# A two-layer hybrid decoder trunk: another order of the heads' projections, single-tile groups at the start, and SP's queue in the planner

## The chip, the cores and the metric

One core of a Trainium2 chip runs the whole program. The metric is the device time in microseconds of one execution. Engine names: PE is TensorE (PEld its weight loads), DVE is VectorE, ACT is ScalarE, POOL is GpSimd, SP is SyncE, on whose queue all loads and stores of this kernel are issued.

## The reference

Sequence 256, width 2048, two layers. For each layer the reference computes

```python
mod = silu(c) @ w_ada[l] + b_ada[l]            # 6 vectors: shift, scale, gate of the mixer, then of the FFN
h = rms_norm(x, ln_mix[l]) * (1 + sc_m) + sh_m
proj = h @ w_in[l]                             # q, k, v, z, b, a of 8 DeltaNet heads; q, k, v of attention
dn_out = gated_deltanet(...)                   # conv, chunked recurrence with a triangular inverse per 64 steps
at_out = sliding_window_attention_sinks(...)   # 16 query heads, 2 key/value heads
x = x + gt_m * (concat(dn_out, at_out) @ w_out[l])
h = rms_norm(x, ln_ffn[l]) * (1 + sc_f) + sh_f
x = x + gt_f * ((silu(gate) * up) @ w_down[l]) # gate, up = h @ w_gate_up[l]
```

and ends with an RMS norm. All inputs are float32.

## The kernel before

x stays in SBUF, transposed: 16 tiles `x[:, k, :]` (k tiles) of 128 channels x 256 positions. Every weight block of 128x128 is split by ACT into a rounded part `wh` and by DVE or POOL into a rest `wl` (`Weights.split`), each activation likewise into two halves (`act`), and a product of a block is three matmuls of 256 columns (`mm3`, for the mixer) or one of 512 and one of 256 (`mm2`, for the FFN and the second product of it).

The order of the work is fixed while the program is built. `Timed` keeps an estimated clock for each engine and prices every recorded instruction; `Steps.run` lets the generators (one for each head, each attention pair, each addition to x) record their next step when the estimate says that its input is there; `Timed.dma` estimates when a load lands, and `Timed.carry` records the small transfers of 8 KB (`qi<-mc`, `uc<-ui`) that rearrange the 16x16 blocks for the inverses. The engines and SP then execute their queues in the recorded order; a step that was recorded too soon makes its engine wait, with all that stands behind it.

The stages, with the names that the change touches:

- **Start of layer 0.** `Ada.products` computes the modulation's shift and scale (m = 0, 1) on PE: loads `wx` of 128x1024, each multiplied in 32-row groups with the columns of silu(c) in `cs`; `finish` turns the result (copy `th`, product with `sel`) and adds it to `mod`. `first_normed` squares x (`kq`), sums the squares (`R`), makes the norm's factor (`ms`, `n2r`, `do`, `ry`), and then for each k tile `gain`, `cv` and the two halves of `act`. Meanwhile 28 early projections (`EARLY`) are accumulated k group by k group (`GROUPS`, now (0, 2), (2, 4), (4, 6), (6, 10)); `keep` stores or adds each partial sum in SBUF. The last group, (10, 16), is done in the next stage. A shift and scale for two k tiles come out of 8 loads.
- **Heads (mix0, mix1).** The projections in the order of `JOBS`: "ak", "av" and "aq" for attention, "k", "q", "v", "z" for the heads. `scores` prepares a head; after the fourth head of a batch (`BATCH` = 4) `inverses` carries `mc` to `qi`, inverts, and carries `ui` to `uc`, 8 transfers each time; `delta` then runs the recurrence of one head, a chain of small products (`con,U`, `W,B`, `y,U`, `U,yn`, `con,vT`, ...) with a DVE or ACT step after each. The projection "v" of head h waits until head h - 2 has got past its `con,vT` step ("mid").
- **Output projection**, with `add_x` adding into x, and the **FFN**. In all stages from the middle of mix0 on, DVE also multiplies the remaining modulation weights (`wada`, `Ada.rows`), 1.2 us for each of 256 loads.

In the order before, each head's k, q and one aq follow each other to the end:

```python
for _h in range(H):
    JOBS += [("v", _h), ("z", _h)]
    for _n in range(BATCH, H):
        if _n - BATCH == _h:
            JOBS += [("k", _n), ("q", _n), ("aq", _n)]
```

Of the kernel before, what the change touches and what calls it, by code (L numbers as in the profile page):

```python
# [23 lines left out]
ALU = mybir.AluOpType  # L24
# [3 lines left out]
KT = D // 128  # L28
# [7 lines left out]
AHEAD, BATCH = 2, 4  # L36
JOBS = [("ak", 0), ("av", 0)] + [("aq", h) for h in range(AHEAD)]
for _h in range(BATCH):
    JOBS += [("k", _h), ("q", _h)] + [("aq", AHEAD + _h // 2)] * (_h % 2)
for _h in range(H):  # L40
    JOBS += [("v", _h), ("z", _h)]
    for _n in range(BATCH, H):
        if _n - BATCH == _h:
            JOBS += [("k", _n), ("q", _n), ("aq", _n)]
# [56 lines left out]
class Timed:  # L101
# [5 lines left out]
    def __init__(self, nc):  # L107
        self.nc, self.floor, self.end, self.count = nc, 0, 0, 0
        self.form = None
        self.clock = {e: 0 for e in ("tensor", "vector", "scalar", "gpsimd")}  # L110
        for e in self.clock:
            setattr(self, e, Engine(self, e))
        self.loads = 0
# [69 lines left out]


JOIN = 4, 2
# [139 lines left out]
class Weights:  # L325
# [60 lines left out]
    def split(self, upto, force=True):  # L386
        nc, b = self.nc, self.b
        while self.nsplit < min(upto, len(self.parts)):
# [3 lines left out]
            eng = "gpsimd" if free and not ffn else "vector"  # L392
# [41 lines left out]
def trunk(tc, xT, bada, c, c_col, par, con, w_in, w_ba, w_ada0, w_ada, w_out, w_gu, w_dn, out):  # L434
    nc = Timed(tc.nc)
    with (
# [38 lines left out]
        for l in range(L):  # L475
            if l == 0:
                for lo, hi in GROUPS[:-1]:
                    n = 8 // (hi - lo)
                    for i in range(0, len(EARLY), n):
                        W.across(w_in[0, i : i + n], lo, hi)  # L480
# [26 lines left out]
        class Ada:  # L507
            BUFS = 3

            def __init__(self):  # L510

                self.todo = [(0, m, j, i) for j in range(8) for m in (1, 0) for i in range(4)]
# [30 lines left out]
            def load(self):  # L543
# [4 lines left out]
                if self.nload < self.cols:  # L548
                    src = w_ada0[COLS.index(m), k, i]
# [5 lines left out]
            def products(self):  # L555
# [3 lines left out]
                for n in range(self.cols):  # L559
                    _, m, j, i = self.todo[n]  # L560
                    size = 1 if m in (1, 0) else 8
                    at = j % size
                    begin, end = i == at == 0, i == 3 and at == size - 1
# [20 lines left out]
                    if end:  # L584
                        self.groups += 1
                        S.add(self.finish(m, j - at, size, to, half), 0)
# [20 lines left out]
            def finish(self, m, j, size, to, half):  # L607
# [6 lines left out]
                for i in range(2):  # L614
# [6 lines left out]
                at = mod[:, 0, m * 16 + 2 * j : m * 16 + 2 * (j + size)].rearrange("p (j i) -> p i j", i=2)  # L621
                nc.vector.tensor_tensor(
                    out=at, in0=at, in1=q[:, 0 : 2 * size].rearrange("p (i j) -> p i j", i=2), op=ALU.add
                )
                b.give("psm")
                self.have.update((0, m, k) for k in range(2 * j, 2 * (j + size)))
# [55 lines left out]
        for n, upto in zip([0] + [len(EARLY) * (hi - lo) // 8 for lo, hi in GROUPS[:-1]], [hi for _, hi in GROUPS]):  # L682
# [233 lines left out]
        def first_normed(x_at, ln, hs):  # L916
            acc = b.t("R", [128, 2, T], bufs=1)
            for i in range(KT // 2):
                yield from b.take("kq", A_)
                nc.floor = max(nc.floor, x_at[i // 2])  # L920
                sq = b.t("kq", [128, 2, T])
                nc.scalar.activation(out=sq, in_=x[:, 2 * i : 2 * i + 2, :], func=AF.Square)
                yield D_
# [4 lines left out]
                b.give("kq")  # L928
# [389 lines left out]
        def inverses(bt, ui):  # L1318
# [8 lines left out]
            nc.end += 7500  # L1327
# [42 lines left out]
            nc.end += 7500  # L1370
# [381 lines left out]
```

## Time and profile before

| | us |
|---|---|
| median of 3 runs | 2565.11 (2564.06 to 2567.55) |
| the profiled execution | 2560.1 |
| its span, first to last instruction | 2558.4 |
| PE busy in the span | 2454.5 |
| DVE / ACT / POOL busy | 1853.5 / 1295.8 / 433.7 |
| mean clock granted to PE | 0.98 of 2.4 GHz |

The profiled execution's time lies 1.7 us above its span and 5.0 us below the median of the runs. The start of layer 0 takes the first 200 us, mix0 lasts to about 505 us, its output projection to 583 us, the FFN to 1335 us, mix1 with its output projection to 1797 us, and the second FFN to the end. "Busy" counts an instruction from its start to its end, at either clock, so time in which PE works at half its clock does not show as idle.

### The profile page before, as it was taken

What the parts mean: (1) busy time and instruction counts of PE and PEld (TensorE: products, weight loads), DVE (VectorE), ACT (ScalarE), POOL (GpSimd) and SP (SyncE); (2) the same over time, 40 slices, a digit from 0 to 9 for tenths busy, and PEclk for the clock granted to TensorE, in tenths of its full rate; (3) what the DMA queues carried; (4) which work ended last, traced back from release to release, by engine and by line L of the source; (5) the groups of instructions that cost most, each with busy time, mean ns of one, the idle gap of its engine ahead of it and who ended that gap; (6) DMA issues with size and microseconds to landing.
All of it is one profiled execution on the core that took longest, in us unless ns stands there. A gap on an engine that the chain in (4) does not pass through costs nothing. (4 is left out here: it accounts for less than half of the span.)

```text
span 2558.4 us, 45650 instructions
## 1 busy us (share of the span) xinstructions
PE 2454.5 (96%) x16878; PEld 2166.9 (85%) x16878; DVE 1853.5 (72%) x3823; ACT 1295.8 (51%) x2760; POOL 433.7 (17%) x389
## 2 busy tenths in 40 slices
PE   6999998988999999999999999899899999999998
PEld 5887787987888888888888899899788888888887
DVE  3758767778777999999987876655877765555565
ACT  4346563535555445555445655454555544555553
POOL 2333232670000000000004333246000000000000
PEclk9999998999999999999999999899999999999999
DMA  9987565776777999999983333346677766555564
GB/s 358 340 300 257 191 231 194 248 267 205 251 256 262 341 354 348 354 349 347 333 293 132 133 130 127 119 160 225 214 255 247 240 190 191 190 190 190 184 189 138
DMA packets 192786, 609.05 MB, mean 238 GB/s; under 512 B 27825, under 2 KB 39217, under 8 KB 192561
## 3 DMA queue, kind: packets, MB, share of 16 engines
q1 hardware_dynamic: 192562, 606.14, 68.8%
q8 instruction: 132, 2.16, 0.3%
q14 instruction: 92, 0.75, 0.1%
HBM read 603.44 MB, written 2.10 MB: 237 GB/s over the span
## 5 line engine op out<-in xcount | busy, mean ns | idle before, releaser
L172 ACT CAST wh<-w 128x512 fp32r<-128x512 f32 x1532 | 896.0, 604 | 475.4 <-PE psm L172 163.0
L172 DVE TENSOR_TENSOR wl<-w,wh 128x512 fp32r<-128x512 f32 (+1 forms) x1293 | 860.8, 683 | 249.7 <-ACT wh L172 237.3
L172 PE MATMUL pr<-act,wh 128*128 128x512 f32 x2816 | 883.5, 394 | 7.6 <-DVE kq L172 4.4
L172 PE MATMUL pm<-act,wh 128*128 128x256 f32 x3328 | 643.5, 293 | 15.6 <-DVE x L172 6.8
L172 PEld LDWEIGHTS pr<-act,wl 128*128 128x128 f32 x2816 | 531.8, 189 | 124.1 <-DVE wl L172 1.4
L172 PE MATMUL pr<-act,wl 128*128 128x256 f32 x2816 | 561.6, 280 | 0.9 <-DVE wl L172 0.9
L172 PEld LDWEIGHTS pm<-act,wh 128*128 128x128 f32 x3328 | 520.9, 192 | 39.0 <-issue 22.7
L172 POOL TENSOR_TENSOR wl<-w,wh 128x512 fp32r<-128x512 f32 (+1 forms) x239 | 331.9, 1398 | 1181.7 <-ACT wh L172 1097.1
L172 PE MATMUL pm<-act,wl 128*128 128x256 f32 x1664 | 474.1, 285 | 0.2 <-POOL wl L172 0.2
L172 PEld LDWEIGHTS pr<-act,wh 128*128 128x128 f32 x2816 | 433.5, 189 | 10.3 <-DVE kq L172 5.0
L172 DVE CUSTOM_DVE_ANT_0 wada<-wada,cs 128x1024 f32<-128x1024 f32 x256 | 330.1, 1290 | 123.0 <-DMA wada<-w_ada 122.8
L172 PE MATMUL psm<-act,wh 128*128 128x512 f32 (+1 forms) x1280 | 363.8, 362 | 1.4 <-DVE act L172 1.2
L172 PEld LDWEIGHTS pm<-act,wl 128*128 128x128 f32 x1664 | 319.5, 192 | 0.4 <-POOL wl L172 0.4
L172 PEld LDWEIGHTS psm<-act,wl 128*128 128x128 f32 x1088 | 205.2, 189 | 39.0
L172 PE MATMUL psm<-act,wl 128*128 128x256 f32 x1088 | 233.3, 281 | 0.0
L172 PEld LDWEIGHTS psm<-act,wh 128*128 128x128 f32 x1280 | 201.4, 189 | 5.8 <-issue 3.7
L172 PE MATMUL psm<-mid,wh 128*128 128x512 f32 x512 | 169.7, 392 | 0.0
L172 POOL TENSOR_TENSOR n2r<-ms,halfc 128x2 f32<-128x2 f32 x5 | 3.5, 690 | 798.4 <-DVE ms L172 798.4
L172 ACT COPY kq<-pr 128x512 f32<-128x512 f32 x88 | 51.4, 587 | 167.2 <-PE pr L172 167.2
L172 PEld LDWEIGHTS psm<-mid,wl 128*128 128x128 f32 x512 | 96.1, 188 | 21.6
L172 DVE TENSOR_TENSOR kq<-pr,kq 128x512 f32<-128x512 f32 x88 | 60.5, 688 | 72.3 <-ACT kq L172 72.3
L172 DVE SCALAR_TENSOR_TENSOR x<-psm,mod,x 128x256 f32<-128x256 f32 x128 | 61.8, 483 | 57.4 <-PE psm L172 54.9
(188 smaller groups left out, 1984.3 us busy)
## 6 DMA issues: line engine op xcount, KB each, us to landing
w<-w_gu SPq DMA_DIRECT2D x352, 512.0 KB
wada<-w_ada SPq DMA_DIRECT2D x320, 512.0 KB
w<-w_in SPq DMA_DIRECT2D x130, 512.0 KB
w<-w_dn SPq DMA_DIRECT2D x128, 512.0 KB
wx<-w_ada SPq DMA_DIRECT2D x64, 512.0 KB
w<-w_out SPq DMA_DIRECT2D x64, 512.0 KB
w<-w_dn SPq DMA_DIRECT2D x64, 384.0 KB
w<-w_in SPq DMA_DIRECT2D x28, 384.0 KB
```

Source lines behind the costliest of these rows:

```text
L172: return f(*a, **k)
```

## The change

It does five things.

1. `JOBS` is written out as a string. Now k, q of the second batch come together sooner (k6 q6 k7 q7 before v3) and aq5, aq6, aq7 stand after z3, between k7 q7 and v4 z4; aq0 and aq1 are no longer both among the first four.
2. `Timed.dma` keeps a time of SP's queue: 400 ns for each load there, and 380 bytes per ns for the transfers in place of 350. `Timed.carry` puts 650 ns on the same queue for each small transfer, and the carried data is there 2000 ns after the last; the fixed 7500 ns after a set of eight are gone.
3. The first modulation goes k tile by k tile: `wx` holds half of the rows for one tile of 128 channels, and a shift and scale for one k tile come out of 4 loads. A load is now multiplied by 8 products of 128 columns (before, 4 of 256). The first four loads are multiplied one by one as they come, later ones four at a time.
4. `GROUPS` begins with (0, 1), (1, 2) in place of (0, 2): two passes over the 28 projections with one k tile each. Their weights come in loads of eight tiles x 128 columns, in pieces of 512 bytes (before, 1 KB).
5. `first_normed` records the squares and their sums without yielding in between, and POOL takes no split before the first product.

```diff
-GROUPS = ((0, 2), (2, 4), (4, 6), (6, 10), (10, 16))
+BATCH = 4
+ORDER = (
+    "ak av aq0 k0 q0 k1 q1 aq1 k2 q2 k3 q3 aq2 aq3 v0 z0 v1 z1 k4 q4 aq4 k5 q5 v2 z2 k6 q6 k7 q7 v3 z3 "
+    "aq5 aq6 aq7 v4 z4 v5 z5 v6 z6 v7 z7 "
+)
+GROUPS = ((0, 1), (1, 2), (2, 4), (4, 6), (6, 10), (10, 16))
...
-        self.loads = max(self.loads, self.clock["tensor"], after) + n / 350
+        self.queue = max(self.queue, self.clock["tensor"], after) + 400
+        self.loads = max(self.loads, self.queue) + n / 380
...
-        self.end = max(self.end, self.floor)
+        self.queue = max(self.queue, self.floor) + 650
+        self.end = max(self.end, self.queue + 2000)
...
-            eng = "gpsimd" if free and not ffn else "vector"
+            eng = "gpsimd" if free and not ffn and self.p else "vector"
...
-                self.todo = [(0, m, j, i) for j in range(8) for m in (1, 0) for i in range(4)]
+                self.todo = [(0, m, k, i) for k in range(KT) for m in (1, 0) for i in range(2)]
...
-                    join = JOIN[n >= self.first]
+                    join = 1 if n < 4 else 4 if early else 2
...
-                    for r in range(4):
-                        c0 = (i * 4 + r) * 32 + 31 - at
+                    size = 128 if early else T
+                    cols = to[:, m * 128 : m * 128 + 128] if early else to
+                    for r in range(1024 // size):
+                        c0 = (i * 1024 // size + r) * 32 + 31 - at
                         nc.tensor.matmul(
-                            to[r * 32 : r * 32 + 32, :], cs[:, c0 : c0 + 32], w[:, r * T : r * T + T], start=begin, stop=end
+                            cols[r % 4 * 32 : r % 4 * 32 + 32, :], cs[:, c0 : c0 + 32], w[:, r * size : r * size + size],
+                            start=(i == 0 and r < 4) if early else begin, stop=(i == 1 and r >= 4) if early else end,
                         )
...
             for i in range(KT // 2):
-                yield from b.take("kq", A_)
-                nc.floor = max(nc.floor, x_at[i // 2])
+                nc.floor = x_at[i // 2]
                 sq = b.t("kq", [128, 2, T])
                 nc.scalar.activation(out=sq, in_=x[:, 2 * i : 2 * i + 2, :], func=AF.Square)
-                yield D_
+                nc.floor = nc.end
...
-            nc.end += 7500
```

Three places on PE show how the order moves. The first is PE's queue from its beginning (`wx` is a load of the modulation, `R` the sum of squares, `do` the norm's factor, `th` the turned row, `act,wh` a projection). Before:

```order
L172 MATMUL psm_111<-wx_93,cs_69 32x256 x4
L172 MATMUL psm_111<-wx_95,cs_69 32x256 x4
L172 MATMUL psm_111<-wx_97,cs_69 32x256 x4
L172 MATMUL psm_111<-wx_99,cs_69 32x256 x4
L172 MATMUL psm_169<-con_67,th_166 128x1 x2
L172 MATMUL psm_172<-con_67,R_112 128x1 x4
L172 MATMUL psm_184<-do_182,con_67 128x256
L172 MATMUL psm_111<-wx_101,cs_69 32x256 x4
L172 MATMUL psm_111<-wx_103,cs_69 32x256 x4
L172 MATMUL psm_111<-wx_105,cs_69 32x256 x4
L172 MATMUL psm_111<-wx_107,cs_69 32x256 x4
L172 MATMUL psm_231<-con_67,th_229 128x1 x2
```

Now:

```order
L172 MATMUL psm_117<-wx_93,cs_69 32x128 x8
L172 MATMUL psm_155<-con_67,R_118 128x1 x4
L172 MATMUL psm_117<-wx_95,cs_69 32x128 x8
L172 MATMUL psm_176<-do_174,con_67 128x256
L172 MATMUL psm_117<-wx_97,cs_69 32x128 x8
L172 MATMUL psm_117<-wx_99,cs_69 32x128 x8
L172 MATMUL psm_213<-con_67,th_203 128x1 x2
L172 MATMUL pm_92<-act_228,wh_205 128x256 x2
L172 MATMUL pm_92<-act_228,wl_206 128x256
L172 MATMUL pm_234<-act_228,wh_205 128x256 x2
```

The norm's products moved in between the first four loads' products, and the first projection stands behind four loads in place of eight.

The second is PE's queue in layer 1 where heads 4 and 5 begin their recurrence (`con,U` is its first step; `act,wh` and `act,wl` are projections). Before:

```order
L172 MATMUL pm_20201<-act_16371,wl_20155 128x256
L172 MATMUL psm_20311<-con_67,U_20305 128x128 x2
L172 MATMUL psm_20314<-con_67,U_20308 128x128 x2
L172 MATMUL psm_20322<-W_20317,B_18116 128x64 x2
L172 MATMUL psm_20325<-W_20319,B_18759 128x64 x2
L172 MATMUL psm_20331<-y_3671_16390,U_20305 128x64
L172 MATMUL psm_20331<-U_20305,y_3671_16390 128x64
L172 MATMUL psm_20331<-y_3671_16390,U_20305 128x64
L172 MATMUL psm_20331<-U_20305,y_3671_16390 128x64
L172 MATMUL psm_20336<-y_3672_16391,U_20308 128x64
L172 MATMUL psm_20336<-U_20308,y_3672_16391 128x64
```

This goes on for 25 more rows of heads 4 and 5 without a projection. Now, for head 4:

```order
L172 MATMUL pm_20151<-act_16423,wl_20035 128x256
L172 MATMUL psm_20182<-con_67,U_20164 128x128 x2
L172 MATMUL pm_20151<-act_16444,wh_20056 128x256 x2
...
L172 MATMUL pm_20151<-act_16555,wl_20081 128x256
L172 MATMUL psm_20219<-W_20199,B_18740 128x64 x2
L172 MATMUL pm_20151<-act_16576,wh_20080 128x256 x2
L172 MATMUL pm_20151<-act_16576,wl_20081 128x256
...
L172 MATMUL pm_20151<-act_16664,wl_20113 128x256
L172 MATMUL psm_20252<-y_3700_16704,U_20164 128x64
L172 MATMUL psm_20252<-U_20164,y_3700_16704 128x64
L172 MATMUL psm_20252<-y_3700_16704,U_20164 128x64
```

Between any two steps of the head stand products of a projection, and head 5 no longer goes in step with head 4. Layer 0 shows the same at its heads 4 and 5.

The third is PE's queue in layer 0 at heads 0 and 1 (`wada,cs` are modulation products). Before, the last projection's product stands in the middle of head 0's steps:

```order
L172 MATMUL pm_3924<-act_2145,wh_3753 128x256 x2
L172 MATMUL pm_3924<-act_2145,wl_3754 128x256
L172 MATMUL psm_111<-wada_3814,cs_69 32x256 x4
L172 MATMUL psm_111<-wada_3915,cs_69 32x256 x4
L172 MATMUL psm_3991<-W_3928,B_2904 32x32 x4
L172 MATMUL pm_3924<-act_2187,wh_3753 128x256 x2
L172 MATMUL pm_3924<-act_2187,wl_3754 128x256
L172 MATMUL psm_4015<-y_480_2196,U_3893 128x64
```

and from the last of these rows on 43 rows have none. Now:

```order
L172 MATMUL pm_4072<-act_2390,wh_3970 128x256 x2
L172 MATMUL pm_4072<-act_2390,wl_3971 128x256
L172 MATMUL psm_4119<-con_67,U_4091 128x128 x2
L172 MATMUL psm_4125<-con_67,U_4097 128x128 x2
L172 MATMUL psm_4137<-w_885_4107,con_67 128x256
L172 MATMUL psm_4137<-w_885_4107,con_67 128x128 x2
L172 MATMUL psm_4141<-W_4129,B_3050 128x64 x2
L172 MATMUL psm_117<-wada_3941,cs_69 32x256 x4
L172 MATMUL psm_117<-wada_4011,cs_69 32x256 x4
L172 MATMUL psm_4159<-W_4144,B_3237 128x64 x2
```

Now the stretch without a projection begins with the first step of both heads and has 61 rows.

## Rows read from the trace of the kernel before

**Rows 1.** The profile page: line 1, the busy time of each engine with its share of the span; then two lines of the span in 40 slices of 64 us, the busy tenths of PE and the clock granted to it in tenths of full speed.

```profile
PE 2454.5 (96%) x16878; PEld 2166.9 (85%) x16878; DVE 1853.5 (72%) x3823; ACT 1295.8 (51%) x2760; POOL 433.7 (17%) x389
...
PE   6999998988999999999999999899899999999998
...
PEclk9999998999999999999999999899999999999999
```

**Rows 2.** The view of windows, one row for each stretch in us: its length, then the busy time of PE, PEld, DVE, ACT and POOL (with the number of instructions), the mean granted clock of PE (1.00 is 2.4 GHz, 0.50 is 1.2 GHz), the DMA share and GB/s. Stretches that the text does not use are left out.

```profile
0.00:37.50 37.50, 16.40 (x97) 9.27 (x97) 13.64 (x29) 12.22 (x23) 5.82 (x9) 0.91 0.96 346
37.50:200.00 162.50, 160.25 (x1579) 138.28 (x1578) 99.38 (x232) 68.20 (x148) 55.42 (x49) 1.00 0.91 328
200.00:425.50 225.50, 212.14 (x1870) 171.60 (x1871) 167.46 (x492) 129.44 (x368) 77.09 (x88) 0.95 0.64 218
425.50:444.00 18.50, 13.27 (x119) 11.24 (x118) 15.55 (x41) 4.40 (x14) 2.61 (x2) 0.63 0.65 233
444.00:583.00 139.00, 129.98 (x1093) 126.03 (x1092) 108.49 (x183) 61.26 (x143) 94.42 (x60) 0.99 0.72 248
...
1643.30:1666.00 22.70, 13.56 (x111) 12.13 (x112) 7.29 (x27) 4.24 (x14) 1.27 (x1) 0.62 0.25 73
...
1797.00:2558.40 761.40, 743.42 (x4240) 649.38 (x4239) 489.99 (x869) 384.94 (x721) 1.38 (x2) 0.99 0.62 202
```

**Rows 3.** The same view for five short stretches of layer 0's heads.

```profile
217.90:221.50 3.60, 1.92 (x30) 1.23 (x28) 2.56 (x6) 2.54 (x7) 0.79 (x1) 1.00 0.98 390
288.20:293.70 5.50, 3.02 (x21) 2.11 (x18) 3.13 (x13) 0.21 (x1) 0.43 (x2) 0.69 0.92 333
386.00:392.80 6.80, 4.91 (x32) 3.92 (x29) 3.96 (x6) 3.32 (x8) 2.21 (x2) 0.75 0.90 328
406.70:413.20 6.50, 4.54 (x20) 3.69 (x19) 5.08 (x18) 1.60 (x4) 1.28 (x1) 0.74 0.65 260
...
299.80:314.39 14.59, 12.02 (x117) 7.67 (x115) 9.58 (x36) 6.92 (x19) 2.42 (x3) 0.77 0.13 48
```

**Rows 4.** The timeline of PE in the first 40 us: start, length in us, engine, line, operation, out<-in, shape, count, and in brackets the idle time before it and what ended it. A float32 product of `wx` or `con` shows as two records.

```profile
14.12 2.25 PE L172 MATMUL psm<-wx,cs 128*32 128x256 f32 x16 [14.12 <-DVE R L172]
...
20.30 1.85 PE L172 MATMUL psm<-con,R 128*128 128x1 f32 x8
23.63 1.22 PE L172 MATMUL psm<-do,con 128*128 128x256 f32 x2 [1.48 <-DVE do L172]
24.78 3.25 PE L172 MATMUL psm<-wx,cs 128*32 128x256 f32 x32
...
30.60 0.38 PE L172 MATMUL pm<-act,wh 128*128 128x256 f32 x1 [1.46 <-ACT act L172]
32.13 0.58 PE L172 MATMUL pm<-act,wh 128*128 128x256 f32 x1 [1.16 <-DVE act L172]
...
34.34 1.10 PE L172 MATMUL pm<-act,wh 128*128 128x256 f32 x2 [1.41 <-ACT act L172]
```

**Rows 5.** PE's groups by form from 40 to 200 us and from 1420 to 1600 us (busy us, mean ns of one record); the answer for the tile `wx`, weight loads (ns min/median/max); and one group of products in the timeline.

```profile
L172 PE MATMUL psm<-wx,cs 128*32 128x256 f32 x416 | 25.1, 382 | 0.0
...
L172 PE MATMUL psm<-w,av 128*64 128x128 f32 x72 | 5.7, 282 | 0.0
...
L172 PEld LDWEIGHTS psm<-wx,cs x512: 105/110/178, 14.1 to 167.7; 128*32 128x32 f32 x171
...
49.45 1.93 PE L172 MATMUL psm<-wx,cs 128*32 128x256 f32 x32
```

**Rows 6.** The timeline of PE in the steady part of the first stage: one product of a 128x128 block by a k tile is three records, two with `wh` and one with `wl`.

```profile
45.04 0.40 PE L172 MATMUL pm<-act,wh 128*128 128x256 f32 x2
...
45.40 0.41 PE L172 MATMUL pm<-act,wh 128*128 128x256 f32 x2
```

**Rows 7.** The timelines of SP's queue, of DVE and of PE where heads 4 and 5 of layer 1 begin their recurrence (length in us after the start).

```profile
1640.72 5.26 SPq L126 DMA_DIRECT2D uc<-ui  x8
...
1647.29 0.43 SPq L121 DMA_DIRECT2D wada<-w_ada  x1
...
1652.27 1.23 DVE L172 CUSTOM_DVE_ANT_0 wada<-wada,cs 128x1024 f32<-128x1024 f32 x1 [7.23 <-DMA wada<-w_ada]
...
1653.76 0.69 PE L172 MATMUL psm<-y,U 128*128 128x64 f32 x2 [7.22 <-DVE y L172]
...
1662.42 0.78 PE L172 MATMUL pm<-act,wh 128*128 128x256 f32 x2
```

**Rows 8.** The view of waits (us in total, times, longest us): PE from 200 to 425 us; DVE from 500 to 590 us; PE from 500 to 583 us; DVE over the whole span.

```profile
PE psm L172 <- DMA wada<-w_ada: 7.2, 5, 2.5
...
DVE wada L172 <- DMA wada<-w_ada: 17.6, 10, 3.7
...
PE pm L172 <- DVE x L172: 6.8, 7, 2.2
...
DVE wada L172 <- DMA wada<-w_ada: 122.8, 65, 7.2
```

**Rows 9.** DVE's groups by form from 60 to 150 us.

```profile
L172 DVE TENSOR_TENSOR act<-psm,act 128x256 f32<-128x256 f32 x41 | 16.6, 418 | 13.1 <-PE psm L172 12.9
```

**Rows 10.** The view of windows for two stretches of the first stage (columns as in Rows 2); up to 20 us all loads are in pieces of 4 KB, after that half of them in pieces of 1 KB.

```profile
8.00:20.00 12.00, 4.90 (x35) 1.41 (x35) 5.27 (x8) 4.97 (x9) 0.00 (x0) 1.00 1.02 399
20.00:60.00 40.00, 34.00 (x282) 28.26 (x282) 18.11 (x39) 18.77 (x43) 11.78 (x9) 0.91 1.06 378
```

More of the change, by code (lines that the diff above doesn't have):

```diff
@@ L32 @@
 NEG = -1e30
[L36 to L44, printed above, removed]
+BATCH = 4
[3 more added lines that the diff above has]
+)
+JOBS = [(job.rstrip("01234567"), int(job[-1]) if job[-1].isdigit() else 0) for job in ORDER.split()]
 EARLY = [(kind, h) for kind, h in JOBS if kind in ("ak", "av", "aq", "k", "q") or (kind == "v" and h < 2)]
 TILES = EARLY + [job for job in JOBS if job not in EARLY]
-GROUPS = ((0, 2), (2, 4), (4, 6), (6, 10), (10, 16))
+GROUPS = ((0, 1), (1, 2), (2, 4), (4, 6), (6, 10), (10, 16))
 FIRST = 10
@@ L112, in __init__ @@
             setattr(self, e, Engine(self, e))
-        self.loads = 0
+        self.loads = self.queue = 0
     def dma(self, out, in_, after=0):
@@ L431, in block, with trunk @@
         return self.cur.pop(0)
-def trunk(tc, xT, bada, c, c_col, par, con, w_in, w_ba, w_ada0, w_ada, w_out, w_gu, w_dn, out):
+def trunk(tc, xT, bada, c, c_col, par, con, w_in, w_ba, w_ada1, w_ada0, w_ada, w_out, w_gu, w_dn, out):
     nc = Timed(tc.nc)
@@ L560, in products @@
                     _, m, j, i = self.todo[n]
-                    size = 1 if m in (1, 0) else 8
-                    at = j % size
-                    begin, end = i == at == 0, i == 3 and at == size - 1
+                    early = n < self.first
+                    at = 0 if early else j % 8
+                    begin, end = (n % 4 == 0, n % 4 == 3) if early else (i == at == 0, i == 3 and at == 7)
                     half = self.groups % 2
                     to = bank[:, half * T : half * T + T]
-                    join = JOIN[n >= self.first]
+                    join = 1 if n < 4 else 4 if early else 2
                     if n % join == 0:
@@ L585, in products @@
                         self.groups += 1
-                        S.add(self.finish(m, j - at, size, to, half), 0)
+                        S.add(self.finish(m, j, to, half, early), 0)
                 while any(self.busy):
@@ L605, in products, with finish @@
                 self.ready = True
-            def finish(self, m, j, size, to, half):
+            def finish(self, m, j, to, half, early):
+                size = 1 if early else 8
                 yield from b.take("th", A_)
@@ L620, in finish @@
                 yield D_
[L621 to L624, printed above, removed]
+                if early:
+                    at = mod[:, 0, j : j + 17 : 16]
+                    nc.vector.tensor_tensor(out=at, in0=at, in1=q[:, 0:2], op=ALU.add)
+                    self.have.update(((0, 0, j), (0, 1, j)))
+                else:
+                    at = mod[:, 0, m * 16 : m * 16 + 16].rearrange("p (j i) -> p i j", i=2)
+                    nc.vector.tensor_tensor(
+                        out=at, in0=at, in1=q[:, 0:16].rearrange("p (i j) -> p i j", i=2), op=ALU.add
+                    )
+                    self.have.update((0, m, k) for k in range(KT))
                 b.give("psm")
-                self.have.update((0, m, k) for k in range(2 * j, 2 * (j + size)))
             def rows(self, n):
@@ L681, in trunk @@
         first, na, nw = [], 0, 0
[L682 removed]
+        units = [-(-len(EARLY) // (8 // (hi - lo))) for lo, hi in GROUPS[:-1]]
+        for n, upto in zip([0] + units, [hi for _, hi in GROUPS]):
             m = upto * 4 - na
```

18 lines of the change are left out of this document (10 added, 8 removed).

## The prediction

> **What bounds the kernel now.** I read the page first: PE is busy for 2454.5 of 2558.4 us, and in the slices the few digits under 9, and the few clock digits under 9, stand at the beginning and in the two head stages [rows 1]. So PE's work is the bound, and a change can win only where PE waits or works at 1.2 GHz. The windows by stage put sizes on that. As the loss of a stretch I take its length less busy time times mean granted clock: 37.5 - 16.4 x 0.91 = 22.6 us at the start; little from 37.5 to 200 us (160 of 162.5 busy at full clock); 18.5 - 13.3 x 0.63 = 10.1 us in the short stretch from 425.5 us; 22.7 - 13.6 x 0.62 = 14.3 us in that from 1643.3 us [rows 2]. The last FFN is busy 743 of 761 us at 0.99: nothing for this change there [rows 2]. Then the timelines and the view of waits show what those stretches wait for, and the order of the instructions shows which of it the change touches.
>
> **The start.** Before, the first projection begins at 30.60 us, after eight products of `wx` [rows 4]. The reader sees the first four from 14.12 us on, then the norm's products (1.85 and 1.22 us, with 1.48 us of waiting between), then the other four until 24.78 + 3.25 = 28.03 us, and 2.57 us later the first projection [rows 4]. Now the other four are off this path. Four products at 2.25 / 2 = 1.1 us, the norm's 1.85 + 1.48 + 1.22 us between them, and 2.57 us behind: 14.12 + 4.5 + 4.6 + 2.6 = 25.8 us, or 4.8 us earlier. The loads for it are the first in the queue as before. The wait for the second k tile (the 1.41 us before 34.34 us) goes as well, because one k tile now feeds 28 projections [rows 4]. What PE saves must stand until the loads of the stage run out: a k tile needs four loads of `wx` and 3.5 of weights, 3.9 MB, which is 10.4 us at 378 GB/s; PE needs 28 x 0.36 us (the pace from 45.04 to 45.40 us) and a group of products of 1.93 us, 12.0 us [rows 5, 6, 10]. PE stays the slower one. Pieces of 512 bytes were not seen here; 4 KB alone ran at 399 GB/s and a mix with 1 KB at 378, so even 10% less makes 11.5 us, still under PE; should they take more, each of the first two k tiles costs the excess, some 2 us [rows 10]. I take 5 us won (2.5 if only the first step's delay is won at half clock, 7 if the clock rises sooner as well). The squares without pauses cost and win nothing: the sums on DVE wait for the last part of x either way, and the first product starts at 14.12 us.
>
> Against that stand the products of 128 columns: 1024 records in place of 512. A group of 32 records of 256 columns takes 1.93 us, 240 ns for each set of four that runs side by side in the array [rows 5]. If 128 columns take half of it, nothing is lost; if they take as long, 16 x 1.93 = 31 us are. The nearest row is `w,av`, 128 columns two side by side: 5.7 us / 72 x 2 = 158 ns for a set, which gives 256 x 158 ns - 128 x 240 ns = 9.7 us [rows 5]. Between 120 and 158 I take 140 ns a set, nearer to the row than to the half: 5 us, with 0 and 10 as ends. On this point a page speaks against the change. The Trainium skill, "TensorE: Matmul & The Clock Gate", section "The mechanism", says that weight loads overlap with running matmuls only if their row groups differ; these all use the same 128 rows, so by the page the 128 further sets would show their loads in full. With the load of 110 ns in the rows that would be 128 x 110 ns = 14 us; the trace disagrees for 256 columns, where a set takes 240 ns, loads included [rows 5]. The partial sums grow by 28 DVE additions of 418 ns, 11.7 us on an engine that is busy for 99 of 162.5 us there: hidden [rows 2, 9]. Without that cover they would cost 11.7 us. The start comes out at 5 - 5 = 0.
>
> **Waits behind the small transfers.** The reader sees the mechanism in layer 1: SP issues eight `uc` transfers for 5.26 us from 1640.72, so the load of `wada` goes out only at 1647.29; DVE has its product already in its queue, waits 7.23 us, and with it wait the head's step behind it and PE (7.22 us) [rows 7]. The planner did not charge SP for these transfers (5.26 / 8 = 0.66 us each); now it charges 0.65. In layer 0 PE itself waits for `wada` (7.2 us, five times) [rows 8]. With the clock the losses by the same formula are 1.7, 3.4, 3.1 and 3.1 us [rows 3], 11.3 in all; the second and the fourth stand right behind such transfers. I take 6 us off, with 0 and 11 as ends. The waits of the output projection (DVE 17.6 us for `wada`, PE 6.8 us for DVE) have no such transfers near and keep their order, so they stay [rows 8].
>
> **Heads 4 and 5.** There before, both heads' chains ran with no projection left beside them, since v6 waits for head 4: no projection until 1662.42 us in layer 1, and the clock fell to 0.62; 14.3 us were lost there and 10.1 in layer 0 [rows 2, 7]. Now v3, z3, aq5, aq6 and aq7 stand between k7 q7 and v4, and the order shows projections between any two steps of head 4 in both layers. I take off 13 and 9.5 us; the rest covers the smaller waits that such a chain always leaves.
>
> **Heads 0 and 1 in layer 0.** In exchange the bare stretch there grows from 43 to 61 rows. It lost 14.59 - 12.02 x 0.77 = 5.3 us [rows 3]. The new one is like that of heads 4 and 5 in layer 0, which lost 10.1, and may in addition wait for `uc`: I add 5 us, with 0 and 10 as ends. POOL's few further splits and the moved aq cost nothing while ACT and DVE are below PE.
>
> **The sum.** 0 - 6 - 13 - 9.5 + 5 = -23.5 us against the profiled execution's 2560.1, so 2536.6; that execution was 5.0 us under the median of the runs, so the median should be 2541 us.
>
> **Rivals.**
>
> *Weight loads bound the new products* (14 us in place of 5). For it: each record has its own load of 105 to 110 ns, and there are twice as many records. Against it: now a set takes 240 ns with its loads [rows 5]. 2541 + 9 = 2550 us. The Trainium skill's page named above is for it too.
>
> *The pause moves and does not go.* The recorded order is the planner's belief. If `uc` comes later than it thinks, PE stands at head 4's first step with the projections behind it in its queue, and the 22.5 us come back. For it: queues run in order, and heads 0 and 1 show that the pause is found elsewhere at once. Against it: there are now five more projections in front. 2541 + 22.5 = 2563.5 us, no change that could be told. So the change would not do what it says.
>
> *DVE waits at the other transfers, and the kernel gets slower.* There are eight sets of eight transfers, and one of them cost 7.2 us before [rows 7]. Loads are now believed to be 8% faster (380 for 350), so products of `wada` are recorded sooner behind them. Four new waits of 7.2 us, 28.8, outweigh the 23.5 that I expect; five give 2541 + 36 = 2577 us. For it: DVE waited 65 times for `wada`, 122.8 us in all, and so many products can be hit [rows 8]. Against it: the planner's 650 ns now agree with the measured 0.66.
>
> **How the numbers follow.** My forecast has a chance of 0.60, with 2530 to 2552 as its own range (ends of the waits and of heads 0 and 1, taken together by halves). Weight loads bound: 0.12. The pause moves: 0.15. DVE waits: 0.10. All waits gone and the products at no cost: 0.03, at 2541 - 5 - 5 - 5 = 2526. A difference under 0.2% (5 us) can't be told from none with this kernel. Faster is then 0.60 + 0.12 + 0.03 and a fifth of the moved pause, 0.78; the same 0.10, most of the moved pause; slower 0.12, DVE waits and the rest of it. The range for 8 in 10 runs from 2524 to 2566: the low end takes all waits gone, the high end the moved pause.
>
> **What would show it.** Right: the first projection near 26 us; sets of `wx` at 140 ns (36 us busy in all); PE without a gap over 2 us at heads 4 and 5 of both layers and its clock at 1.00 there; no wait of DVE for `wada` behind `uc`. Wrong: a `wx` group over 2.6 us; a gap before the first `con,U` of heads 0 or 4 over 5 us; PE idle between 40 and 150 us for loads; or half clock in other stretches of the heads, as long in sum as those that went.

## The result, and the profile of the changed kernel

The changed kernel takes 2540.28 us (median of 4 runs, 2535.20 to 2545.64), the kernel before beside it 2564.59 us (4 runs, 2560.74 to 2567.55). The ratio is 0.9905, with a 95% interval of 0.9887 to 0.9923: 24.3 us faster, where the forecast was 2541 us. The profiled execution took 2543.46 us, 3 us over its median, while that of before lay 5 us under its own; so the two spans, 2558.4 and 2541.8 us, show only 16.6 us of the 24.3.

The page of the changed kernel, the lines of [rows 1]:

```profile
PE 2447.7 (96%) x17390; PEld 2169.2 (85%) x17390; DVE 1872.0 (74%) x3843; ACT 1294.5 (51%) x2762; POOL 444.2 (17%) x395
...
PE   6999999998999999999999999999999999999998
...
PEclk9999999998999999999999999999999999999999
```

PE's work is the bound as before, and no clock digit is under 9 any more in the two head stages. The windows that answer to [rows 2] (columns as there; the ends of the stages have moved; the first row is the kernel before, from 40 to 76 us, the others are the changed kernel):

```profile
40.00:76.00 36.00, 36.00 (x348) 32.81 (x347) 18.36 (x42) 18.42 (x42) 15.67 (x12) 1.00 1.03 367
...
40.00:76.00 36.00, 31.41 (x370) 28.83 (x370) 27.00 (x60) 13.12 (x29) 13.66 (x10) 0.91 1.03 367
200.00:425.00 225.00, 211.93 (x1952) 170.91 (x1951) 177.79 (x505) 127.52 (x366) 83.81 (x94) 0.99 0.67 224
425.00:440.00 15.00, 14.33 (x115) 12.44 (x116) 12.63 (x31) 8.64 (x28) 4.01 (x4) 1.00 0.41 147
...
1640.00:1660.00 20.00, 19.91 (x189) 18.71 (x188) 13.34 (x34) 13.10 (x39) 6.58 (x5) 1.00 0.39 136
```

The reader sees three things. The short stretch of heads 4 and 5 is now 14.33 of 15 us busy at full clock in layer 0, and 19.91 of 20 in layer 1, where 10.1 and 14.3 us were lost [rows 2]. The stretch from 200 us has a clock of 0.99 for 0.95. And there is a new bad stretch at the start: from 40 to 76 us PE is busy for 31.41 of 36 us, at 0.91, where before it had no gap (36.00 of 36 us); DVE is busy there for 27.00 us, before for 18.36.

To see where the time went, both programs are cut where PE's work is the same. The 281st product with `act,wl` (28 projections x 10 k tiles are 280) ends the part that I call start, the 672nd (42 x 16 are 672 in all) the projections of mix0; then come the first product of the first FFN, the norm of layer 1 (`do,con`), the first product of the second FFN, and the end. Lengths in us, worked out from the starts of these records in the profiled executions; the times are medians, with the ratio to the kernel before, which was run beside each (`after_again` is the changed kernel once more). Apart from `wx`, PE's recorded products in each part are the same before and now, but for 6 that stand on the other side of a cut:

| kernel | start | mix0 | to FFN | FFN 0 | mix1 | FFN 1 | median | ratio, 95% interval |
|---|---|---|---|---|---|---|---|---|
| before | 174.9 | 302.6 | 113.3 | 747.1 | 463.8 | 756.8 | 2564.59 | 1 |
| changed | 179.2 | 291.2 | 110.8 | 750.3 | 451.2 | 759.1 | 2540.28 | 0.9905, 0.9887 to 0.9923 |
| order_only | 176.3 | 301.8 | 111.7 | 746.9 | 447.6 | 756.8 | 2551.16 | 0.9939, 0.9918 to 0.9959 |
| est_only | 173.4 | 307.2 | 112.9 | 750.2 | 460.2 | 753.9 | 2559.43 | 0.9975, 0.9961 to 0.9988 |
| start_only | 180.7 | 313.6 | 112.0 | 747.6 | 463.0 | 757.9 | 2580.62 | 1.0053, 1.0033 to 1.0072 |
| old_start | 173.5 | 293.2 | 111.7 | 746.9 | 448.4 | 762.1 | 2538.19 | 0.9888, 0.9870 to 0.9907 |
| after_again | 178.8 | 293.0 | 110.4 | 750.1 | 449.7 | 760.1 | 2540.18 | 0.9896, 0.9878 to 0.9914 |
| groups_136 | 174.5 | 292.4 | 112.5 | 749.4 | 449.2 | 758.9 | 2537.98 | 0.9886, 0.9867 to 0.9906 |
| groups_old | 171.9 | 293.0 | 110.8 | 748.2 | 448.8 | 756.1 | 2534.63 | 0.9876, 0.9859 to 0.9894 |
| pool_off | 172.3 | 294.6 | 112.4 | 744.1 | 447.5 | 758.7 | 2531.53 | 0.9867, 0.9850 to 0.9884 |
| pool_off_old | 170.5 | 292.4 | 110.5 | 750.2 | 449.9 | 757.3 | 2532.52 | 0.9870, 0.9846 to 0.9894 |
| pool_off_136 | 171.2 | 294.1 | 112.5 | 751.8 | 449.0 | 753.4 | 2533.26 | 0.9877, 0.9859 to 0.9895 |
| old_start_pool_off | 173.1 | 290.7 | 110.7 | 754.2 | 450.5 | 757.3 | 2535.67 | 0.9880, 0.9861 to 0.9899 |
| pool_none | 171.9 | 301.7 | 103.5 | 752.6 | 435.7 | 756.7 | 2524.23 | 0.9841, 0.9822 to 0.9860 |

The changed kernel won 11.4 us in mix0 and 12.6 in mix1, and lost 4.3 in the start. The FFN columns scatter by 10 us among kernels that do the same work there, so differences of a few us in a single profile mean nothing; the start column and the mix columns stand out of that where kernels with the same part agree (start: 178.8, 179.2 and 180.7 with all of the new start; 170.5 to 176.3 otherwise).

The start in PE's timeline, as in [rows 4]:

```profile
14.68 1.08 PE L172 MATMUL psm<-wx,cs 128*32 128x128 f32 x16 [14.68 <-DMA wx<-w_ada]
...
17.49 1.08 PE L172 MATMUL psm<-wx,cs 128*32 128x128 f32 x16
...
20.19 1.94 PE L172 MATMUL psm<-wx,cs 128*32 128x128 f32 x32
...
25.79 0.58 PE L172 MATMUL pm<-act,wh 128*128 128x256 f32 x1 [2.16 <-ACT act L172]
...
33.53 1.96 PE L172 MATMUL psm<-wx,cs 128*32 128x128 f32 x64
```

The first projection begins at 25.79 us, with four loads' products before it. The rate of the products of 128 columns (columns as in [rows 5]):

```profile
L172 PE MATMUL psm<-wx,cs 128*32 128x128 f32 x896 | 28.8, 284 | 0.0
...
L172 PEld LDWEIGHTS psm<-wx,cs x1024: 106/110/178, 14.7 to 167.2; 128*32 128x32 f32 x171
```

A group of 64 records (the last row of the timeline) takes 1.96 us, 16 sets of four at 122 ns: twice the records in the time of before [rows 5]. Then PE loses what it has won. One such place, from the timeline of DVE, POOL and PE:

```profile
54.69 1.30 POOL L172 TENSOR_TENSOR wl<-wy,wh 128x512 fp32r<-128x512 f32 x1 [3.09 <-ACT wh L172]
...
54.84 1.70 DVE L172 TENSOR_TENSOR wl<-wy,wh 128x512 fp32r<-128x512 f32 x1
...
56.64 0.48 DVE L172 SCALAR_TENSOR_TENSOR cv<-x,gain,ry 128x256 f32<-128x256 f32 x1
57.05 1.08 DVE L172 TENSOR_TENSOR act<-pm,act 128x256 f32<-128x256 f32 x3
...
58.04 0.74 DVE L172 TENSOR_TENSOR act<-psm,act 128x256 f32<-128x256 f32 x2
...
58.51 0.50 PE L172 MATMUL psm<-act,wh 128*128 128x256 f32 x2 [1.87 <-DVE act L172]
...
58.78 1.74 POOL L172 TENSOR_TENSOR wl<-w,wh 128x512 fp32r<-128x512 f32 x1 [2.79 <-ACT wh L172]
...
59.30 1.50 DVE L172 SCALAR_TENSOR_TENSOR act<-cv,mod,act 128x256 fp32r<-128x256 f32 x1
...
60.73 1.07 DVE L172 TENSOR_TENSOR act<-psm,act 128x256 f32<-128x256 f32 x3
```

PE stands for 1.87 us until 58.51, for a sum that DVE has to take out of its bank of PSUM, the memory that PE writes its sums to: the two additions listed at 58.04 run one after the other, and the first of them ends at 58.45. DVE is late because its split `wl` at 54.84 took 1.70 us, beside a split on POOL from 54.69 to 55.99. At 59.30 the second half of an act takes 1.50 us, beside POOL's split of 58.78 to 60.52, and the additions behind it begin only at 60.73. Half clock from 59.4 to 66.2 us followed these waits.

SP's queue at `uc` of layer 1, and the waits that answer to [rows 7, 8] (DVE for `wada` in all; PE for `wada` from 200 to 425 us; DVE and PE in the output projection):

```profile
1592.58 5.28 SPq L125 DMA_DIRECT2D uc<-ui  x8
...
DVE wada L172 <- DMA wada<-w_ada: 116.1, 58, 5.1
...
PE psm L172 <- DMA wada<-w_ada: 4.2, 8, 0.8
...
DVE wada L172 <- DMA wada<-w_ada: 11.5, 9, 5.1
...
PE pm L172 <- DVE x L172: 4.2, 4, 1.9
```

The eight `uc` transfers still take 5.28 us, but no wait of DVE stands behind them. The waits for `wada` in all went only from 122.8 to 116.1 us, and PE's for it in layer 0 from 7.2 to 4.2.

### The profile page after: what moved, and what is told of

Same layout as the page of the kernel before. It is cut to its first block, busy times and chain, and to the rows that moved or that the text cites. A ratio compares the mean times of both kernels' runs of the same rounds, so it can differ in the third digit from the quotient of the medians.

```text
span 2541.8 us, 46725 instructions
## 1 busy us (share of the span) xinstructions
PE 2447.7 (96%) x17390; PEld 2169.2 (85%) x17390; DVE 1872.0 (74%) x3843; ACT 1294.5 (51%) x2762; POOL 444.2 (17%) x395
## 5 line engine op out<-in xcount | busy, mean ns | idle before, releaser
L172 POOL TENSOR_TENSOR wl<-w,wh 128x512 fp32r<-128x512 f32 (+1 forms) x245 | 343.5, 1411 | 1141.0 <-ACT wh L172 1066.0
L172 DVE CUSTOM_DVE_ANT_0 wada<-wada,cs 128x1024 f32<-128x1024 f32 x256 | 332.1, 1298 | 116.1 <-DMA wada<-w_ada 116.1
```

Source lines behind the costliest of these rows:

```text
L172: return f(*a, **k)
```

## The experiments

The theory after this profile (O): the order makes the gain, the estimate some of it, and the start costs. The rivals: that the estimate makes it (E), and that the start wins and the later 281st product comes from elsewhere (S).

**order_only**: the kernel before with the new `ORDER`, `BATCH` and `JOBS`, nothing else.

```diff
-AHEAD, BATCH = 2, 4
-JOBS = [("ak", 0), ("av", 0)] + [("aq", h) for h in range(AHEAD)]
...
+JOBS = [(job.rstrip("01234567"), int(job[-1]) if job[-1].isdigit() else 0) for job in ORDER.split()]
...
```

> The kernel before with the new order of the heads' projections alone (old estimate, old start). Theory O: the order carries most of the gain, since in the trace after the stretches of heads 4 and 5 lost their pauses: layer 1's mixer is 12.3 us shorter there and layer 0's 11.4, of which the estimate has some 4; so 17 to 22 us under before, about 2545. Rival E: it is the estimate that takes PE's waits away, and the order alone is recorded so that PE stands at heads 4 and 5 all the same: within 6 us of before.

Measured: 2551.16 us beside 2567.67, so 16.5 under, just short of Theory O's 17 to 22. But the whole gain lies in layer 1 (mix1 447.6 for 463.8 us); mix0 is as long as before. Windows of layer 0 (twice) and layer 1, a row of PE's timeline, and two of SP's queue:

```profile
396.00:414.00 18.00, 15.00 (x99) 13.02 (x98) 6.59 (x23) 6.21 (x18) 2.01 (x2) 0.72 0.60 207
425.00:440.00 15.00, 14.93 (x122) 12.68 (x120) 11.54 (x25) 10.74 (x33) 3.66 (x3) 1.00 0.51 168
1640.00:1660.00 20.00, 19.08 (x181) 17.75 (x180) 13.71 (x41) 12.66 (x41) 7.61 (x6) 1.00 0.41 126
...
403.18 1.08 PE L169 MATMUL psm<-wada,cs 128*32 128x256 f32 x8 [3.00 <-DMA wada<-w_ada]
...
390.15 6.90 SPq L123 DMA_DIRECT2D uc<-ui  x8
...
397.65 0.85 SPq L118 DMA_DIRECT2D wada<-w_ada  x2
```

Heads 4 and 5 run full in both layers (14.93 of 15, 19.08 of 20), yet before them in layer 0 PE now stands 3.00 us for `wada`, whose load SP issued only at 397.65, behind the eight `uc` transfers, and with the half clock behind it the stretch from 396 us has 15.0 of 18 us busy at 0.72. With the old estimate, then, layer 0's pause moved and did not go.

**est_only**: the kernel before with the new `dma` and `carry` and without the 7500 ns.

```diff
-        self.loads = max(self.loads, self.clock["tensor"], after) + n / 350
+        self.queue = max(self.queue, self.clock["tensor"], after) + 400
+        self.loads = max(self.loads, self.queue) + n / 380
...
```

> The kernel before with the new estimate of SP's queue alone. Theory O: the wait of DVE behind the uc transfers of layer 1 (7.23 us) goes, but heads 4 and 5 stay without projections, so some 2 to 7 us under before, about 2560, and half clock stays at heads 4 and 5. Rival E: 15 us or more under before, with full clock at heads 4 and 5.

Measured: 2559.43 us, 8.2 under before by the medians and 6.4 by the ratio, about Theory O's upper end and half of what E asked. The stages do not show where: in the table mix0 is 4.6 us longer than before and mix1 3.6 shorter, and the two profiled spans differ by 0.6 us (2557.8 for 2558.4). The windows show why it is no more: heads 0 and 1 (first row) run at 0.63, heads 4 and 5 of layer 0 at 0.60 and of layer 1 at 0.76.

```profile
290.00:322.00 32.00, 28.12 (x207) 20.86 (x206) 15.11 (x67) 13.31 (x44) 4.24 (x4) 0.63 0.32 96
425.00:446.00 21.00, 14.61 (x115) 11.95 (x113) 18.04 (x48) 4.32 (x13) 1.33 (x1) 0.60 0.60 191
1640.00:1668.00 28.00, 22.62 (x197) 20.80 (x196) 16.86 (x42) 8.50 (x23) 3.09 (x3) 0.76 0.32 97
```

**start_only** and **old_start**: the kernel before with the new start alone, and the changed kernel with the old start.

```diff
-GROUPS = ((0, 2), (2, 4), (4, 6), (6, 10), (10, 16))
+GROUPS = ((0, 1), (1, 2), (2, 4), (4, 6), (6, 10), (10, 16))
...
-                self.todo = [(0, m, j, i) for j in range(8) for m in (1, 0) for i in range(4)]
+                self.todo = [(0, m, k, i) for k in range(KT) for m in (1, 0) for i in range(2)]
...
```

> The kernel before with the new start alone (first modulation k tile by k tile, single-tile groups, squares without pauses). Theory O: the start loses, as in the trace after, where the 281st projection product ends 4.3 us later than before: 3 to 6 us over before, about 2569, with the first projection at about 25.8 us and PE waiting for act between 48 and 72 us. Rival S: the start wins the 4.8 us by which the first projection comes earlier, about 2560, and the later place of the 281st product is due to the other parts.

> The changed kernel with the old start (new order and new estimate alone). Theory O: 3 to 6 us under the changed kernel, about 2536. Rival S: 5 us over the changed kernel, about 2545.

Measured: the new start alone makes the kernel 13.0 us slower (2580.62 for 2567.67 us), more than expected: 5.9 us in the start itself, and mix0 is 11 us longer than before, with waits for `wada` of up to 4.2 us. That the old estimate misplaces the loads after this start is likely, but no run shows it by itself. Without the new start the changed kernel takes 2538.19 us; the 2 us to the changed kernel can't be told by the times (the intervals overlap), but the start is 5.7 us shorter (173.5 for 179.2). Rival S falls. With order and estimate together both layers' heads run full, and mix0 is 293.2 us long, where order and estimate alone left 301.8 and 307.2 (windows of the place where order_only stood, and of heads 4 and 5 of both layers):

```profile
396.00:414.00 18.00, 17.94 (x199) 13.87 (x199) 8.93 (x36) 8.48 (x28) 3.58 (x3) 1.00 0.51 178
422.00:437.00 15.00, 14.33 (x116) 12.43 (x115) 12.96 (x30) 8.70 (x28) 4.37 (x3) 1.00 0.43 150
1635.00:1655.00 20.00, 19.91 (x189) 18.71 (x188) 14.25 (x35) 12.92 (x39) 5.61 (x5) 1.00 0.41 137
```

In layer 0 the two parts are worth something only together.

The next runs asked why the new start loses. Theory D: the additions of the extra passes stand in DVE's queue; P: DVE's steps are slow beside POOL's splits; L: loads come late; M: the products themselves.

**groups_136**, **groups_old**, **pool_off**, and the changed kernel again:

```diff
-GROUPS = ((0, 1), (1, 2), (2, 4), (4, 6), (6, 10), (10, 16))
+GROUPS = ((0, 1), (1, 3), (3, 6), (6, 10), (10, 16))              # groups_136
+GROUPS = ((0, 2), (2, 4), (4, 6), (6, 10), (10, 16))              # groups_old
...
-            eng = "gpsimd" if free and not ffn and self.p else "vector"
+            eng = "gpsimd" if free and not ffn and u >= self.marks["mix0"] else "vector"   # pool_off
```

> The changed kernel with the groups (0,1), (1,3), (3,6), (6,10), (10,16): the first pass still has one k tile, but there are four passes of partial sums as before, not five, so 28 additions of DVE fewer. Theory D (the start loses because these additions stand in DVE's queue before the act that PE waits for): PE's waits for act between 40 and 76 us go, the 281st projection product ends at 171 to 175 us in place of 179.2, and the kernel takes 2533 to 2537 us. Rival L (the start loses because loads of wx come late, SP standing at their buffers): as the changed kernel, 179 us and 2540 us.

> The changed kernel with the groups of before ((0,2) first), its modulation still k tile by k tile. Theory D: no waits for act between 40 and 76 us either; the first projection still at about 26 us; the 281st product at 171 to 175 us. Rival M (products of 128 columns and single-tile modulation are the cause): 179 us as in the changed kernel.

> The changed kernel without splits on POOL before the last group, so DVE does all of them there. Theory P (DVE's own steps are slow beside POOL: an act half took 1.50 us where POOL ran and 0.50 us elsewhere, and that is what PE waits for): DVE's act halves take 0.5 us each, the waits between 40 and 76 us go, 281st product at 171 to 175 us. Theory D: DVE has some 12 splits of 0.7 us more in those 50 us, so the waits grow; 281st product later than 179 us, and the kernel 2542 to 2550 us.

> The changed kernel once more, beside the three others on one chip: 24 us under before (2540 us where before takes 2565), with PE's waits for act between 40 and 76 us and the 281st product at 178 to 181 us.

Measured: 2537.98, 2534.63, 2531.53 and 2540.18 us. Theory P is the one that hit in numbers: with POOL off the start takes 172.3 us, and all 4 runs (2529.51 to 2533.45) lie under all 5 of the changed kernel (2536.13 to 2543.78), although DVE does all splits. Since the planner prices every engine, these runs also record a somewhat different order. For pool_off, the window from 40 to 76 us and DVE's groups in it:

```profile
40.00:76.00 36.00, 34.20 (x458) 31.30 (x458) 29.06 (x76) 14.95 (x32) 0.00 (x0) 1.00 1.06 382
...
L172 DVE TENSOR_TENSOR wl<-wy,wh 128x512 fp32r<-128x512 f32 x9 | 6.1, 688 | 3.5 <-ACT wh L172 3.3
...
L172 DVE SCALAR_TENSOR_TENSOR act<-cv,mod,act 128x256 fp32r<-128x256 f32 x4 | 1.9, 478 | 0.0
```

and for the changed kernel beside it:

```profile
40.00:76.00 36.00, 31.39 (x371) 28.83 (x370) 26.76 (x60) 12.89 (x28) 13.65 (x10) 0.91 1.05 374
...
L172 DVE TENSOR_TENSOR act<-psm,act 128x256 f32<-128x256 f32 x21 | 7.6, 412 | 0.0
...
L172 DVE SCALAR_TENSOR_TENSOR act<-cv,mod,act 128x256 fp32r<-128x256 f32 x4 | 4.6, 1161 | 0.0
L172 DVE TENSOR_TENSOR wl<-wy,wh 128x512 fp32r<-128x512 f32 x3 | 3.8, 1254 | 1.8 <-ACT wh L172 1.8
```

The act halves take 478 for 1161 ns, the splits of `wy` 688 for 1254. The additions, which read one input from PSUM, take 412 ns even with POOL running. DMA works as hard in both (1.06 and 1.05), so L falls; M falls with groups_old, which keeps the products of 128 columns and has the start in 171.9 us. Theory D's prediction for pool_off (later than 179 us) missed, yet fewer passes help as well, and there the starts lie in D's range of 171 to 175 us: groups_old lies under after_again in all runs (2530.62 to 2535.73), while groups_136 with 2537.98 us is 1 us over D's range and can't be told from after_again by its times. In groups_136 the start is 4.4 us shorter than in after_again, and the wait that is left is one of P's:

```profile
46.01 1.38 POOL L172 TENSOR_TENSOR wl<-w,wh 128x512 fp32r<-128x512 f32 x1 [0.29 <-ACT wh L172]
46.20 1.48 DVE L172 SCALAR_TENSOR_TENSOR act<-cv,mod,act 128x256 fp32r<-128x256 f32 x1
...
47.73 0.58 PE L172 MATMUL pm<-act,wh 128*128 128x256 f32 x1 [3.43 <-DVE act L172]
```

DVE's half of an act takes 1.48 us beside POOL's split, and PE waits 3.43 us for it until 47.73. Here PE waits for the act itself; in the changed kernel it waits for additions that stand behind such a step, which my expectation had put wrongly.

**pool_off_old**, **pool_off_136**, **old_start_pool_off**, **pool_none**: POOL's splits off in the start with each of the two other groupings, with the old start (on new order and estimate), and POOL's splits off everywhere.

```diff
-            eng = "gpsimd" if free and not ffn and self.p else "vector"
+            eng = "gpsimd" if free and u < 0 else "vector"          # pool_none
```

> The changed kernel without POOL's splits in the start and with the groups of before ((0,2) first). Theory P (DVE's steps stretched beside POOL make act late; the single-tile groups only make that chain tight): with POOL off the groups matter little, 281st product at 170 to 173 us, the kernel 2528 to 2533 us, within 3 us of the run with POOL off alone. Theory D (the additions themselves cost): 5 us under it, 2525 to 2527 us.

> The changed kernel without POOL's splits in the start and with the groups (0,1), (1,3), (3,6), (6,10), (10,16). Theory P: the wait of 3.43 us for act at 44.30 us goes, 281st product at 169 to 173 us, the kernel 2527 to 2533 us. Theory D: as the groups alone, 174.5 us and 2538 us, or worse, since DVE has more to do.

> The new order and estimate with the old start, without POOL's splits in the start. Theory P: the old start has two k tiles of work before each act is due and hardly waits for act, so POOL's absence gives it little: 281st product at 172 to 174 us, the kernel 2535 to 2539 us; the new start with POOL off (2531.5 us) is then the better one by 4 to 7 us, as much as the earlier first projection. Rival Q: POOL's absence is a gain of its own for any start, because wada and wl on DVE run faster too: 2530 us.

> The changed kernel with all splits on DVE, in the start and in both head stages. If only the collision counts, DVE's steps run at their short length everywhere and the kernel takes 2525 to 2532 us. If DVE's load counts (it is busy for 89 of 100 us from 200 to 300 us), the some 200 splits of 0.69 us more make DVE late in the heads: start as with POOL off (281st product at 172 us), but the two head stages 5 to 30 us longer, 2537 to 2560 us.

Measured: 2532.52, 2533.26, 2535.67 and 2524.23 us. With POOL off the grouping no longer matters (2531.5 to 2533.3 us, starts of 170.5 to 172.3), and Theory P holds against D; pool_off_136 came out 0.3 us above its range. The old start hardly gains (2535.67 for 2538.19, a start of 173.1 for 173.5): there too DVE's steps are stretched (in the kernel before 9 of the 16 act halves of the start overlap a split on POOL, and take 1.49 us in the median), but PE rarely waits for them. The new start with POOL off is 1 to 3 us shorter than the old one, not the 4.8 by which its first projection is earlier; the medians differ by 4.1 us, with overlapping intervals.

pool_none is the fastest of all, 41 us under before. Its page, the windows of mix0 and of the output projection, and two groups of DVE:

```profile
PE 2448.7 (97%) x17390; PEld 2175.8 (86%) x17390; DVE 1899.8 (75%) x4105; ACT 1296.7 (51%) x2762; POOL 77.1 (3%) x133
...
171.95:473.67 301.73, 282.97 (x2483) 233.10 (x2482) 225.06 (x674) 163.72 (x460) 33.83 (x56) 0.94 0.65 216
461.00:572.00 111.00, 110.31 (x941) 108.51 (x940) 102.79 (x220) 55.87 (x123) 2.07 (x3) 1.00 0.88 299
...
L172 DVE CUSTOM_DVE_ANT_0 wada<-wada,cs 128x1024 f32<-128x1024 f32 x256 | 311.9, 1219 | 93.4 <-DMA wada<-w_ada 93.1
...
L172 DVE SCALAR_TENSOR_TENSOR act<-cv,mod,act 128x256 fp32r<-128x256 f32 x64 | 30.6, 478 | 0.6 <-ACT act L172 0.6
```

The window of mix0 and the same two groups in the changed kernel:

```profile
179.16:470.33 291.17, 275.29 (x2527) 225.06 (x2526) 230.16 (x635) 164.68 (x471) 108.52 (x113) 0.99 0.68 227
...
L172 DVE CUSTOM_DVE_ANT_0 wada<-wada,cs 128x1024 f32<-128x1024 f32 x256 | 332.1, 1298 | 116.1 <-DMA wada<-w_ada 116.1
...
L172 DVE SCALAR_TENSOR_TENSOR act<-cv,mod,act 128x256 fp32r<-128x256 f32 x64 | 46.1, 720 | 1.0 <-ACT act L172 1.0
```

262 splits moved from POOL to DVE (395 less 133 instructions). The durations of DVE's splits sum to 157 us more, those of its other steps to 106 us less (20 of it `wada`, 15.5 the act halves), summed over all its records in the two traces; its busy time rose only from 1872.0 to 1899.8 us. So two thirds of what POOL took off DVE came back as stretched steps. The output projection takes 103.5 for 110 us and mix1 435.7 for 450. The time is 0.8 us under the range of the first theory (only the collision counts). But mix0 (301.7) is 7 to 11 us longer than in the kernels of the table that share its order and estimate, with PE at a clock of 0.94 and one wait of 4.57 us for DVE at 436.2. That DVE's load does this, the second theory, is not shown: DVE is busy for 225.06 us in that window and for 230.16 in the changed kernel, and where most of the half clock falls, at heads 0 and 1 (0.70 from 280 to 320 us), it is busy for 26.4 of 40 us. The part is not quite the same either, since 44 products of the head chains now stand behind its end. Why mix0 is longer stays open. POOL's splits in mix0 alone might be better still; that wasn't run.

## Why the prediction was right, and where it was not

The time (2541 for 2540.28 us) and its likeliest case held. The terms did not all do so.

- **First projection**: 25.8 us forecast, 25.79 measured. The hit is luck in part: the first product comes 0.56 us later (14.68 for 14.12, waiting for its load), the last stretch from the `wx` products to the projection takes 3.66 us for 2.57, and the products before it take as much less (7.45 us from the first product to the end of the last `wx`, for the 9.1 of the sum).
- **Products of 128 columns**: 5 us forecast at 140 ns a set; 122 ns measured, so nothing, the low end of the range. In the start PE is busy with `wx` for 34.75 us before and 34.90 now. The rule of the Trainium skill, "TensorE: Matmul & The Clock Gate", section "The mechanism", by which these loads would show in full, does not describe this: with loads of 110 ns a set took half of the 240 ns of before, to within 2 ns. The same section of the Trainium skill also lets a load run ahead of running products where it goes to a background weight buffer, which the prediction left out; 122 ns would fit that, but no run here shows the buffer. The rival fell with the 122 ns.
- **The start as a whole**: 0 forecast, 4.3 us lost. The 281st product ends 4.3 us later although the first projection begins 4.8 earlier, so 9.1 us went in between. From 40 us to the end of the start PE waits 5.1 us for DVE (1.1 before), and half clock ran for 6.8 us in the middle of these waits. The step that failed is "hidden" for the additions, and the balance of a single-tile pass, which I drew up for PE against the loads only. DVE's 99 of 162.5 us was an average over the stage. In the pass itself an addition occupies DVE for 0.33 us (three from 57.05 on, the next at 58.04) and PE produces a sum each 0.36 us [rows 6]; with splits and acts beside that DVE was busy for 17.5 of 20 us from 42 us on. The runs with fewer passes and with POOL off both gave the time back. In pool_off all 28 further additions are still there and the start is 172.3 us; so the additions are hidden where DVE's steps are short, and what the sum left out is that POOL's splits stretch them.
- **Waits behind small transfers**: 6 us forecast, from windows of layer 0; the estimate alone gave 8.2, which agrees in number only, since in layer 0 it won nothing by itself (mix0 307.2 for 302.6). The wait of 7.23 us behind `uc` in layer 1 went. In layer 0 8.6 us (301.8 to 293.2) came when the estimate was added to the new order.
- **Heads 4 and 5**: 13 us in layer 1 forecast; mix1 is 12.6 us shorter in the changed kernel and 16.2 with the order alone, so the size was right. In layer 0 forecast for all of mix0 were 6 + 9.5 - 5 = 10.5 us; 11.4 came.
- **Heads 0 and 1 in layer 0**: 5 us of loss forecast, none came: the clock stayed full from 209.6 to 574.8 us in spite of 61 rows without a projection. That does not hold for every kernel with this order: pool_none has a clock of 0.70 there.
- **The formula for losses** overstates what can be won. By it mix0 lost 34.5 us before and 17.6 after (idle time plus half of the busy time at half clock), 17 us less, of which heads 4 and 5 have 9.4, the 9.5 of the forecast (10.1 before, 0.7 in the window now); the time fell by 11.4. The rest, PE's busy time for the same products counted at full clock, grew by 5.5 us, and in the sum that stood in for the 5 us of heads 0 and 1. Whether small products lose less than half at half clock, or cost more between projections, no run tells apart.
- **The moved pause** (0.15) was real: order_only shows it in layer 0. What avoided it is the estimate, which I had counted as a term of its own and not as the condition of the other.
- **DVE waits at other transfers**: not seen; 58 waits for `wada`, the longest 5.1 us, for 65 and 7.2.
- **Output projection and FFN**: the waits stayed in the main, as forecast (DVE 11.5 us for 17.6, PE 4.2 for 6.8). That they are not a matter of loads alone shows in pool_none.

So the two head terms were right in sum, and errors of opposite sign did the rest: 5 us not paid for the products, 9.1 lost in the start after a first projection that came 4.8 earlier, and 5.5 us of longer busy time in the place of the 5 at heads 0 and 1. The agreement to 1 us is luck beyond that. The three parts with forecast terms (start, mix0, mix1) fell by 19.7 us in the profiled executions and the whole span by 16.6, where the medians fell by 24.3; the difference no run places. The executions of the changed kernel alone differ by 10 us, and the sum itself gives 2541.6.

## What to carry to other kernels

Draw up the balance of a short pass for every engine that it uses, in that pass, and not from a stage's average: halving the work per pass doubles the partial sums per unit of time. Where two parts of a change meet in one queue, ask whether one is the condition of the other; alone, order and estimate were worth nothing in layer 0, together 9 us. And work moved to POOL is not free for DVE when both read SBUF: look at DVE's durations beside POOL's before counting it as help.

## What the runs showed of the hardware

A DVE step with both large inputs in SBUF waits for POOL's: the act half took 0.48 us alone and 1.50 beside a split (59.30 us, ending 0.28 us after POOL's), a split 0.68 and 1.70, a `wada` product 1.22 on average without POOL and 1.30 with it; additions with one input from PSUM took 0.41 us either way. When a stretched step ends depends on POOL's end and not on its own start: in the start of the changed kernel all 19 of these steps that took over 0.9 us end 0.28 to 0.29 us (act halves) or 0.55 us (splits) after POOL's split. It goes the other way too: of POOL's 36 splits of 128x512 there, 28 take 1.28 to 1.31 us, and the eight that take 1.40 to 1.82 each began while a split or an act half of DVE was under way. The Trainium skill, "SBUF — State Buffer", section "Who interferes with whom", states this: a VectorE instruction with two SBUF inputs contends with a GpSimd instruction that reads SBUF, and the later one blocks until the other ends. The trace agrees, with those numbers. The prediction did not price it, since it counted POOL only as an engine with room. And sets of four products side by side took 122 ns for 128 columns after 240 for 256, weight loads of 110 ns included.
